# The low half of each weight tile made by an accumulating GpSimd transfer

## The chip, the cores and the metric

The kernel runs on one core of a Trainium2 chip. The metric is device time in microseconds (us). Before the change the median of three runs is 882.69 us (882.68 to 883.96).

## The reference

One decoder layer on x of shape (1, 512, 1024), float32:

```
xn = rmsnorm(h, norm1_gain)
q, k, v, u, gates = split(xn @ w_in)              # 1024+1024+1024+512+2048 columns
o  = diff_attention(rope(rmsnorm(q)), rope(rmsnorm(k)), v)   # 8 heads, causal, softmax - lam*softmax
attn_branch = (rmsnorm(o) * 0.8) @ w_attn_proj
s  = s5_layer(u, ...)                             # 32 groups, state 64, scan over 512 tokens, GLU
ssm_branch = s @ w_ssm_proj
h  = h + (g_attn * attn_branch + g_ssm * ssm_branch) @ w_out     # gates through a sigmoid
hn = rmsnorm(h, norm2_gain)
gate, val = split(causal_dwconv(hn @ w_up))       # 2 x 2816 columns, convolution of width 3
h  = h + (silu(gate) * val) @ w_down
```

## The kernel before

Every large product is done in three passes of TensorE, so that float32 accuracy is kept with the fast `float32r` type. An operand a is split into a high half, a rounded to `float32r`, and a low half, a minus that. The product is then high times high, low times high and high times low (`mm3`, lines 536 to 539). Activations are split by `split` (lines 541 to 543); weights are split by `split_w` (lines 520 to 528), which is what changes here.

A weight comes from HBM in pieces of 512 KB, 128 partitions by 1024 floats (four pieces of `w_down` are 256 KB). `load_raw` (508 to 518) takes a buffer from a ring of three (`wr`) and issues one DMA on SyncE's queue. `split_w` takes a buffer from a ring of four for the high half (`wh`) and one from a ring of four for the low half (`wl`). Then:

```
S.copy(hi, raw)
V.tensor_sub(lo, raw, hi.bitcast(F32))
```

ScalarE (S) writes the high half with a rounding copy. VectorE (V) subtracts it from the raw piece and writes the low half. The raw buffer is free for the next load when the subtraction is done; the buffers of the halves are free when TensorE has used them. There are 134 pieces: 44 of `w_in` (the first two of q and of k, split at lines 658 and 660, come first in the kernel), 2 of the GLU, 4 of `w_ssm_proj`, 8 of `w_attn_proj`, 8 of `w_out`, 44 of `w_up` and 24 of `w_down`.

The layer runs in this order, with much overlap: norm 1 and the first projections (up to about 90 us); the state-space layer, its constants and the first attention heads (about 90 to 230 us), where GpSimd does the products of `s5_const`, `s5_chunk`, the rotary step and the inverse square roots, and VectorE the scans, the softmax steps and many eliminations of PSUM; the other heads and the gates (to about 410 us); the mixing and `w_out` (to about 515 us); the gated feed-forward with its convolution (to about 765 us); and `w_down`.

The order is not written by hand. `Schedule` records every operation with its engine, its price (`price`) and what it depends on; `solve` (320 to 419) is a list scheduler that plays the engines through with these prices, and picks on each engine, among the operations whose inputs and buffers are ready, the one with the longest tail plus a constant for its phase (`boost`, lines 465 to 474). `emit` writes the instructions in that order. On the chip each engine works through its own list in order, so an instruction whose input is late holds up all that stands behind it on its engine. The queue of SyncE carries all loads and stores; GpSimd issues no DMA before the change. `shared_port` tells the planner which GpSimd and VectorE operations exclude each other.

Of the kernel before, what the change touches and what calls it, by code (L numbers as in the profile page):

```python
# [8 lines left out]
F32 = mybir.dt.float32  # L9
F32R = mybir.dt.float32r  # L10
AF = mybir.ActivationFunctionType
ALU = mybir.AluOpType
# [68 lines left out]

class Op:
    __slots__ = ("lock", "eng", "calls", "cost", "preds", "succs", "tiles", "alloc", "prio", "npred", "ready", "idx", "start",
                 "end", "nbytes", "phase", "tail", "left", "sim")


class Schedule:
# [3 lines left out]
           "POOL": {"POOL": 30.0, "DVE": 60.0, "ACT": 75.0, "PE": 150.0}}  # L91
    DMA_BW = 355.0
    COLD = 16500.0

    def __init__(self, nc):
        self.nc = nc
# [59 lines left out]
    def _init(self, o, eng):  # L156
        o.eng, o.calls, o.cost, o.preds, o.succs, o.tiles, o.alloc = eng, [], 0.0, {}, [], set(), []
        o.nbytes = 0
        o.lock = False
        o.phase = self.phase  # L160
        o.idx = len(self.ops)
# [85 lines left out]
    @staticmethod  # L247
    def shared_port(eng, fn, out, ins):

        if eng == "POOL":  # L250
            return fn != "memset"
        if eng != "DVE":
            return False
        sb = sum(1 for x in ins if not str(x.space).endswith("PSUM") and x.free_size() > 1)
        return sb > 1 or (sb == 1 and fn in ("tensor_copy", "tensor_scalar"))
# [8 lines left out]
    def price(self, eng, fn, out, ins, acc, o):  # L264
        n = 1
        for x in out.shape[1:]:
            n *= x
        if eng == "PE":
            if fn == "transpose":
                return 109.0  # L270
            if ins[-1].dtype == F32R:
                c = max(0.4167 * n + 13.5, 98.0 if tuple(ins[0].ap)[-1][0] == 1 else 246.0)

                return c if ins[0].shape[0] > 64 else c / 2
            return 1.667 * n + 11 if out.shape[0] > 32 else 55.0
        ps = any(str(x.space).endswith("PSUM") for x in ins)
        ptr = sum(1 for x in ins[1:] if x.free_size() == 1 and n > 1)
        if eng == "ACT":
            return (50 if ps else 92) + 0.833 * n + 93 * ptr + (93 if acc is not None else 0)
        if eng == "DVE":  # L280
            if fn == "reciprocal":
                return 67 + 8 * n
            if fn == "tensor_tensor_scan":
                return 68 + 2.083 * n
            if fn == "tensor_reduce":
                m = 1
                for x in ins[0].shape[1:]:
                    m *= x
                return 68 + 1.042 * m
            ops = sum(1 for x in ins if x.free_size() > 1 or n == 1)  # L290
            if fn in ("tensor_copy", "tensor_scalar", "memset") and not ps:
                return 68 + 0.521 * n
            ptr = sum(1 for x in ins[1:] if x.free_size() == 1) if fn == "scalar_tensor_tensor" else 0
            return 68 + 1.042 * n + (60 if ptr else 0)
        if eng == "POOL":
            if any(v is ALU.pow for v in [o.calls[-1][2].get("op")]):
                return 300 + 165 * n
            if fn == "memset":
                return 36 + 0.84 * n
            if fn == "tensor_copy":  # L300
                return 120 + 3.35 * n
            return 150 + (1.66 if out.shape[-1] <= 16 else 2.1) * n
        o.nbytes += n * out.shape[0] * 4
        return 460.0


    def rank(self):
        for o in self.ops:
            for p in o.preds:
                p.succs.append(o)  # L310
        for o in reversed(self.ops):
            dur = o.cost + (1900.0 + o.nbytes / self.DMA_BW if o.eng == "SP" else 0.0)
            o.tail = dur + max([s.tail + self.lat(o, s) for s in o.succs], default=0.0)

    def lat(self, a, b):
        if a.eng == "SP":
            return 0.0
        return self.LAT[a.eng].get(b.eng, 130.0)

    def solve(self):  # L320
# [5 lines left out]
        left = {t: t.left for o in ops for t in o.alloc}  # L326
# [29 lines left out]
        now = 0.0  # L356
        while done < len(ops):
            if not events:
                self.stuck(ops, avail, waiting, can, used, tagused)
            now = heapq.heappop(events)  # L360
            while events and events[0] <= now + 1e-6:
                heapq.heappop(events)
            while pend and pend[0][0] <= now + 1e-6:
                _, _, o = heapq.heappop(pend)
# [5 lines left out]
            for e in engs:  # L370
                if free_at[e] > now + 1e-6:
                    continue
                w = waiting[e]
                while w and w[0][0] <= now + 1e-6:
                    _, i = heapq.heappop(w)
                    heapq.heappush(avail[e], (-ops[i].prio, i))
                hold = []
                pick = None
                while avail[e]:
                    pr, i = heapq.heappop(avail[e])  # L380
                    if can(ops[i]):
                        pick = ops[i]
                        break
                    hold.append((pr, i))
                for h in hold:
                    heapq.heappush(avail[e], h)
                if pick is None:
                    if w:
                        heapq.heappush(events, w[0][0])
                    continue  # L390
                o = pick
                for t in o.alloc:
                    used[t.cls] = used.get(t.cls, 0) + 1
                    tagused[t.tag] = tagused.get(t.tag, 0) + 1
                    nxt[t.cls] = max(nxt.get(t.cls, 0), t.seq + 1)
                o.start = now
                cost = o.cost * (2.0 if e == "PE" and now < self.COLD else 1.0)
                if o.lock:
                    cost += max(0.0, port - now)
                    port = now + cost  # L400
                free_at[e] = now + cost
                o.end = now + cost
                if e == "SP":
                    dma_free = max(now + 1100.0, dma_free) + o.nbytes / self.DMA_BW
                    o.end = dma_free + 900.0
                heapq.heappush(events, free_at[e])
                heapq.heappush(events, o.end)
                heapq.heappush(pend, (o.end, o.idx, o))
                for s in o.succs:
                    s.npred -= 1  # L410
                    r = o.end + self.lat(o, s)
                    s.ready = max(s.ready, r)
                    if s.npred == 0:
                        heapq.heappush(waiting[s.eng], (s.ready, s.idx))
                        heapq.heappush(events, s.ready)
                order.append(o)
                done += 1
# [21 lines left out]
def build(tc, A, out, dbg=None):  # L439
# [11 lines left out]
    def bc(ap, shape):  # L451
# [10 lines left out]
    sch.caps = {"X": 10, "N": 19, "C": 29, "T": 8, "Z": 15, "S": 18, "G2": 23, "sT": 25, "g": 10, "R": 26,  # L462
        "rope": 33, "P": 15, "AT": 15, "O": 8, "pmm": 3, "pa": 2, "px": 1, "po": 1, "p5": 4, "pu": 4, "pq": 9, "pb": 7}

    sch.boost = {"": 6384700, "c0": -125100, "c1": -423900, "c2": 861800, "c3": -573000, "down0": 4913100,
# [5 lines left out]
        "s3": 5910300, "ssm": -676100, "swk": 2750200, "swq": -2342100, "tables": 482600, "u": 1182300,  # L471
# [3 lines left out]
    sch.fifo = set(sch.caps) | {"wr", "wh", "wl", "F", "cv", "h", "mS", "hr"}  # L475
    sch.dram = {"hbuf": {}, "sbuf": {}}

# [39 lines left out]
            raws.append(raw)  # L517
        return raws

    def split_w(raws):  # L520
        res = []
        for raw in raws:
            hi = sch.new_tile(wpool.tile(list(raw.shape), F32R, tag="wh", name=nm("wh"), bufs=4), "wh", "wh")
            lo = sch.new_tile(wpool.tile(list(raw.shape), F32R, tag="wl", name=nm("wl"), bufs=4), "wl", "wl")
            S.copy(hi, raw)
            V.tensor_sub(lo, raw, hi.bitcast(F32))
            res.append((hi, lo))
        return res

# [110 lines left out]
    for t in range(NT):  # L640
# [14 lines left out]
            split(xh[c], xl[c], pb.rearrange("p (k n) -> p k n", k=4))  # L655
        if t == 1:
            sch.phase = "swq"
            w_q = split_w(raw_q)
    sch.phase = "swk"
    w_k = split_w(raw_k)  # L660

    sch.phase = "tables"

# [769 lines left out]
```

## Time and profile before

| What | Value |
|---|---|
| median of three runs | 882.69 us |
| the profiled execution's own time | 883.83 us |
| its span, first to last instruction | 882.1 us |
| TensorE matmul (PE) busy | 853.6 us, 97% |
| VectorE (DVE) busy | 585.9 us, 66% |
| ScalarE (ACT) busy | 363.8 us, 41% |
| GpSimd (POOL) busy | 181.9 us, 21% |
| DMA engines, mean busy share | 32% |
| granted TensorE clock, mean | 0.992 |

A busy time is the time in which at least one instruction of that engine ran. The clock is the share of full speed that was granted to TensorE; it is either full or half at any moment. The share of the DMA engines is a mean over the core's 16. Since every operation is emitted at line 436, rows are told apart by their tiles: `wr`, `wh` and `wl` are the raw piece and its halves, `pb` a PSUM bank, `s_S` and `s_T` the work tiles of the state-space layer, `k` its constants, `s_P` the softmax tiles, `s_cv` the convolution tiles of the feed-forward.

### The profile page before, as it was taken

Reading aid. Unit: us, or ns where it says so; the run is one execution under the profiler, and the core shown is the slowest. Engines: PE = TensorE matmul, PEld = TensorE weight load, DVE = VectorE, ACT = ScalarE, POOL = GpSimd, SP = SyncE. Lnnn points to the kernel's source line nnn. Section 1 sums busy time; section 2 is a strip of 40 time slices with the busy share of each in tenths; the row PEclk is TensorE's granted clock in tenths of the full one; section 3 lists DMA queues with packets and bytes.
Section 4 is the critical chain, followed back from the end, with each engine's and each line's share of the span. In section 5 each row is a group of like instructions: output and inputs, shape, how many; then the busy total and the mean of one; then the engine's idle time right before and its main releaser. Section 6 shows DMA issues by size and latency. Waiting matters only on the chain.

```text
span 882.1 us, 12703 instructions
## 1 busy us (share of the span) xinstructions
PE 853.6 (97%) x4922; PEld 738.9 (84%) x4922; DVE 585.9 (66%) x1129; ACT 363.8 (41%) x703; POOL 181.9 (21%) x169
## 2 busy tenths in 40 slices
PE   5999899989899999999999999999999999999998
PEld 3998679979679989888889988888888888888887
DVE  4668999899995788864444532599877777324322
ACT  5325462643552466654132531464444444213210
POOL 2445686226103304200000000012211111000000
PEclk9999999989999999999999999999999999999999
DMA  9131113113142301228332652433333333322321
GB/s 286 31 117 49 49 48 94 51 49 97 50 137 91 115 17 49 72 71 273 100 100 85 207 171 76 118 95 96 96 96 95 96 98 99 103 69 86 119 84 59
DMA packets 113208, 85.95 MB, mean 97 GB/s; under 512 B 9634, under 2 KB 99322, under 8 KB 113148
## 3 DMA queue, kind: packets, MB, share of 16 engines
q1 hardware_dynamic: 113148, 85.14, 31.6%
q8 instruction: 38, 0.62, 0.3%
q14 instruction: 22, 0.18, 0.1%
HBM read 78.84 MB, written 6.29 MB: 97 GB/s over the span
## 4 chain that ended last, share of the span: by engine, by line
PE 83%; DVE 10%; ACT 3%; issue 2%; DMA 1%; SPq 1%; POOL 0%; DVEq 0%; ACTq 0%
PE pb L436 83%; DVE s_S L436 4%; DVE wl L436 1%; DVE k L436 1%; DVE s_P L436 1%; DMA s_X<-in_x 1%; ACT s_P L436 1%; DMA wr<-in_w_in 1%; DVE s_rope L436 1%; SPq L436 1%; DVE ml L436 1%; ACT s_G L436 0%; ACT k L436 0%; DVE s_G L436 0%; ACT s_g L436 0%
## 5 line engine op out<-in xcount | busy, mean ns | idle before, releaser
L436 ACT CAST wh<-wr 128x1024 fp32r<-128x1024 f32 (+1 forms) x134 | 139.2, 1039 | 330.1 <-PE pb L436 290.6
L436 DVE TENSOR_TENSOR wl<-wr,wh 128x1024 fp32r<-128x1024 f32 (+1 forms) x134 | 172.3, 1290 | 153.0 <-ACT wh L436 152.6
L436 PE MATMUL pb<-hh,wh 128*128 128x512 f32 (+1 forms) x368 | 140.4, 382 | 0.9 <-ACT wh L436 0.9
L436 PE MATMUL pb<-hh,wl 128*128 128x512 f32 (+1 forms) x368 | 139.8, 380 | 0.0
L436 PE MATMUL pb<-hl,wh 128*128 128x512 f32 (+1 forms) x368 | 139.8, 380 | 0.0
L436 PE MATMUL pb<-wh,xh 128*128 128x256 f32 (+1 forms) x416 | 125.7, 302 | 0.0
L436 PE MATMUL pb<-wh,xl 128*128 128x256 f32 (+1 forms) x416 | 122.2, 294 | 0.1
L436 PE MATMUL pb<-wl,xh 128*128 128x256 f32 (+1 forms) x416 | 122.0, 293 | 0.0
L436 POOL TENSOR_TENSOR s_cv<-s_cv,s_cv 128x512 f32<-128x512 f32 x22 | 37.6, 1707 | 263.1 <-DVE s_cv L436 235.9
L436 PEld LDWEIGHTS pb<-wh,xh 128*128 128x128 f32 x416 | 84.3, 203 | 2.9 <-issue 1.0
L436 PEld LDWEIGHTS pb<-wh,xl 128*128 128x128 f32 x416 | 84.3, 203 | 0.7 <-DVE xl L436 0.4
L436 PEld LDWEIGHTS pb<-wl,xh 128*128 128x128 f32 x416 | 84.2, 202 | 0.0
L436 PEld LDWEIGHTS pb<-hh,wh 128*128 128x128 f32 x368 | 69.2, 188 | 14.2 <-ACT wh L436 1.0
L436 PEld LDWEIGHTS pb<-hh,wl 128*128 128x128 f32 x368 | 69.2, 188 | 13.4 <-issue 0.2
L436 PEld LDWEIGHTS pb<-hl,wh 128*128 128x128 f32 x368 | 69.2, 188 | 13.2
L436 PE MATMUL pb<-wh,s_F 128*128 128x512 f32 (+1 forms) x252 | 71.5, 370 | 0.0
L436 DVE SCALAR_TENSOR_TENSOR s_cv<-s_cv,cw,s_cv 128x511 f32<-128x511 f32 (+1 forms) x88 | 67.7, 805 | 0.0
L436 POOL TENSOR_TENSOR s_T<-k 128x256 f32<-128x256 f32 (+1 forms) x48 | 48.8, 1049 | 22.9 <-DVE k L436 22.9
L436 PEld LDWEIGHTS pb<-wh,s_F 128*128 128x128 f32 x252 | 45.4, 188 | 8.6
L436 PE MATMUL pb<-xh,wh 128*128 128x512 f32 x128 | 52.6, 411 | 0.0
L436 ACT ACTIVATE s_P<-s_P,mx,rq 128x128 f32<-128x128 f32 (+3 forms) x64 | 41.3, 649 | 24.1 <-DVE mx L436 24.1
L436 PE MATMUL pb<-xl,wh 128*128 128x512 f32 x128 | 50.1, 392 | 0.0
(207 smaller groups left out, 1632.1 us busy)
## 6 DMA issues: line engine op xcount, KB each, us to landing
wr<-in_w_in SPq DMA_DIRECT2D x44, 512.0 KB
wr<-in_w_up SPq DMA_DIRECT2D x44, 512.0 KB
wr<-in_w_down SPq DMA_DIRECT2D x20, 512.0 KB
wr<-in_w_attn_proj SPq DMA_DIRECT2D x8, 512.0 KB
wr<-in_w_out SPq DMA_DIRECT2D x8, 512.0 KB
s_X<-in_x SPq DMA_DIRECT2D x8, 256.0 KB
wr<-in_w_ssm_proj SPq DMA_DIRECT2D x4, 512.0 KB
sbuf<-s_g SPq DMA_DIRECT2D x8, 256.0 KB
```

Of the source, the lines that this page charges most:

```text
L436: getattr(e, fn)(*a, **k)
```

## The change

The low half is made in two steps for 130 of the 134 pieces. ScalarE, right behind the high half, writes the negated high half into the low half's buffer: the raw piece times -1, rounded in the same way. GpSimd then issues a DMA that adds the raw piece, in place, onto that buffer. VectorE's subtraction is gone there. The four first pieces of q and k keep it (`split_w(..., False)`). The planner gets a price for the new operation: 1.1 us of GpSimd to issue it, and 3.5 us more until the data has landed; its loads are planned as if the new transfers took nothing from the DMA engines. All phase constants are different, so the order of the whole kernel is drawn anew. Rings and sizes are the same.

```diff
-    def split_w(raws):
+    def split_w(raws, dma=True):
         ...
             S.copy(hi, raw)
-            V.tensor_sub(lo, raw, hi.bitcast(F32))
+            if dma:
+
+                S.mul(lo, raw, -1.0)
+                G.dma_start(lo, raw, accum_op=ALU.add)
+            else:
+                V.tensor_sub(lo, raw, hi.bitcast(F32))
...
-            w_q = split_w(raw_q)
+            w_q = split_w(raw_q, False)
...
-    w_k = split_w(raw_k)
+    w_k = split_w(raw_k, False)
...
+    ADD_ISSUE = 1100.0
+    ADD = 3500.0
...
-            return fn != "memset"
+            return fn not in ("memset", "dma_start")
...
         if eng == "POOL":
+            if fn == "dma_start":
+                o.post = self.ADD
+                return self.ADD_ISSUE
...
-                o.end = now + cost
+                o.end = now + cost + o.post
...
-    sch.boost = {"": 6384700, "c0": -125100, "c1": -423900, "c2": 861800, "c3": -573000, "down0": 4913100,
...
+    sch.boost = {"": 3729900, "c0": 18900, "c1": -112300, "c2": -298700, "c3": -1460600, "down0": 5137100,
...
```

## Rows read from the trace of the kernel before

**Rows 1.** Page, part 1: busy us of each engine, share of the span, instructions.
```profile
PE 853.6 (97%) x4922; PEld 738.9 (84%) x4922; DVE 585.9 (66%) x1129; ACT 363.8 (41%) x703; POOL 181.9 (21%) x169
```

**Rows 2.** All engines in four stretches of the span.
```profile
core 0: us, PE busy (x) PEld busy (x) DVE busy (x) ACT busy (x) POOL busy (x), PEclk, DMA share, GB/s
...
92.40:228.70 136.30, 123.11 (x883) 110.21 (x881) 129.03 (x224) 60.69 (x137) 73.83 (x72) 0.96 0.22 66
...
564.70:882.10 317.40, 313.17 (x1437) 260.46 (x1435) 196.21 (x239) 116.57 (x144) 37.55 (x22) 1.00 0.30 93
...
0.00:20.00 20.00, 9.74 (x36) 6.44 (x36) 8.53 (x12) 10.58 (x19) 3.92 (x14) 1.00 0.94 304
...
862.00:882.10 20.10, 16.75 (x97) 14.51 (x96) 4.23 (x7) 1.24 (x2) 0.00 (x0) 0.97 0.14 53
```

**Rows 3.** What PE waited for between 92.4 and 228.7 us: total, times, longest.
```profile
PE pb L436 <- DVE s_S L436: 5.8, 5, 1.9
PE pb L436 <- DVE s_P L436: 2.4, 1, 2.4
```

**Rows 4.** PE alone: stretch, its length, busy (count), granted clock, DMA share, GB/s.
```profile
175.00:180.00 5.00, 2.71 (x23) 1.00 0.00 0
180.00:185.00 5.00, 3.19 (x14) 0.62 0.00 0
```

**Rows 5.** Low halves on DVE: stretch, its length, busy (count), clock, DMA share, GB/s.
```profile
92.40:228.70 136.30, 22.25 (x16) 0.96 0.22 66
...
470.20:860.00 389.80, 91.44 (x69) 1.00 0.34 105
```

**Rows 6.** Page, part 5: groups with busy us, mean ns of one, idle before.
```profile
L436 ACT CAST wh<-wr 128x1024 fp32r<-128x1024 f32 (+1 forms) x134 | 139.2, 1039 | 330.1 <-PE pb L436 290.6
L436 DVE TENSOR_TENSOR wl<-wr,wh 128x1024 fp32r<-128x1024 f32 (+1 forms) x134 | 172.3, 1290 | 153.0 <-ACT wh L436 152.6
```

**Rows 7.** Timeline of ACT (start, duration): a high half in the state-space stage.
```profile
175.86 1.05 ACT L436 CAST wh<-wr 128x1024 fp32r<-128x1024 f32 x1 [0.25 <-PE pb L436]
```

**Rows 8.** Timeline of DVE: the low half of that same piece.
```profile
199.42 1.22 DVE L436 TENSOR_TENSOR wl<-wr,wh 128x1024 fp32r<-128x1024 f32 x1
```

**Rows 9.** Timeline of the feed-forward: high halves, a low half, the next load.
```profile
642.39 1.05 ACT L436 CAST wh<-wr 128x1024 fp32r<-128x1024 f32 x1 [1.72 <-PE pb L436]
...
643.48 1.82 DVE L436 TENSOR_TENSOR wl<-wr,wh 128x1024 fp32r<-128x1024 f32 x1 [0.41 <-ACT wh L436]
...
645.33 11.24 SPq L436 DMA_DIRECT2D wr<-in_w_up  x3
...
647.79 1.05 ACT L436 CAST wh<-wr 128x1024 fp32r<-128x1024 f32 x1 [2.92 <-PE pb L436]
...
658.67 1.05 ACT L436 CAST wh<-wr 128x1024 fp32r<-128x1024 f32 x1 [2.92 <-PE pb L436]
```

**Rows 10.** Timeline: a load, and the copy that waited for it.
```profile
114.76 3.14 SPq L436 DMA_DIRECT2D wr<-in_w_in  x2
...
118.27 1.05 ACT L436 CAST wh<-wr 128x1024 fp32r<-128x1024 f32 x1 [2.01 <-DMA wr<-in_w_in]
```

**Rows 11.** DMA queue between 640 and 660 us: packets, MB, share of 16 engines.
```profile
q1 hardware_dynamic: 4160, 2.10, 36.0%
```

**Rows 12.** Chain of waits (start, us, what): an early load.
```profile
3.82 5.29 DMA wr<-in_w_in
```

**Rows 13.** Instructions on `wr` (min/median/max ns): one DMA issue on SyncE's queue.
```profile
L436 SPq DMA_DIRECT2D wr<-in_w_up x44: 367/368/385, 483.1 to 721.5; - x44
```

**Rows 14.** Groups of the whole run: POOL's, and one of ACT.
```profile
L436 POOL TENSOR_TENSOR s_T<-k 128x256 f32<-128x256 f32 (+1 forms) x48 | 48.8, 1049 | 22.9 <-DVE k L436 22.9
...
L436 ACT ACTIVATE s_cv<-s_cv,cw 128x512 f32<-128x512 f32 x44 | 35.8, 814 | 18.7 <-DVE s_cv L436 18.7
...
L436 POOL TENSOR_TENSOR dtxe<-ecol,k 128x16 f32<-128x16 f32 x1 | 3.3, 3345 | 1.8 <-DVE qss L436 1.8
```

**Rows 15.** DVE between 92.4 and 228.7 us: tensor-scalar steps on SBUF tiles.
```profile
L436 DVE TENSOR_SCALAR s_S<-s_S 128x512 f32<-128x512 f32 x8 | 3.4, 419 | 0.3 <-ACT s_S L436 0.3
```

More of the change, by code (lines that the diff above doesn't have):

```diff
@@ L83 @@
     __slots__ = ("lock", "eng", "calls", "cost", "preds", "succs", "tiles", "alloc", "prio", "npred", "ready", "idx", "start",
-                 "end", "nbytes", "phase", "tail", "left", "sim")
+                 "end", "nbytes", "post", "phase", "tail", "left", "sim")
 class Schedule:
@@ L158, in _init @@
         o.nbytes = 0
+        o.post = 0.0
         o.lock = False
@@ L311, in rank @@
         for o in reversed(self.ops):
-            dur = o.cost + (1900.0 + o.nbytes / self.DMA_BW if o.eng == "SP" else 0.0)
+            dur = o.cost + o.post + (1900.0 + o.nbytes / self.DMA_BW if o.eng == "SP" else 0.0)
             o.tail = dur + max([s.tail + self.lat(o, s) for s in o.succs], default=0.0)
     def lat(self, a, b):
-        if a.eng == "SP":
+        if a.eng == "SP" or a.post:
             return 0.0
@@ L463, in build @@
         "rope": 33, "P": 15, "AT": 15, "O": 8, "pmm": 3, "pa": 2, "px": 1, "po": 1, "p5": 4, "pu": 4, "pq": 9, "pb": 7}
-    sch.boost = {"": 6384700, "c0": -125100, "c1": -423900, "c2": 861800, "c3": -573000, "down0": 4913100,
[5 rows of a table removed]
-        "s3": 5910300, "ssm": -676100, "swk": 2750200, "swq": -2342100, "tables": 482600, "u": 1182300,
[3 rows of a table removed]
+    sch.boost = {"": 3729900, "c0": 18900, "c1": -112300, "c2": -298700, "c3": -1460600, "down0": 5137100,
[5 rows of a table added]
+        "s3": 5370100, "ssm": 199700, "swk": 2188400, "swq": -3373700, "tables": 1028600, "u": 2523400,
[3 rows of a table added]
     sch.fifo = set(sch.caps) | {"wr", "wh", "wl", "F", "cv", "h", "mS", "hr"}
```

16 rows, old and new, of the table psum are left out of this document.

## The prediction

> **What bounds the kernel now.** I read the page's first part, then busy times by stretch, then what PE waits for, then the timelines. PE is busy 853.6 us of a span of 882.1 [rows 1], so 28.5 us are all that PE ever idles. The stretches say where: 10.3 us in the first 20, where the first loads come in; 3.4 us in the last 20, after the last matmul; 13.2 us between 92.4 and 228.7 [rows 2]. Everywhere else together there are 1.6. From 564.7 us on, feed-forward and `w_down`, PE idles 4.2 us, nearly all in the tail, and no faster VectorE helps there.
>
> The stretch from 92.4 to 228.7 us is the one that the change can reach. There DVE is busy 129.0 of 136.3 us, POOL 73.8 and ACT 60.7 [rows 2]. PE's waits are for DVE: 5.8 us on state-space tiles, 2.4 on softmax tiles, the rest in smaller ones down to 0.6 [rows 3]. They cost a second time: between 175 and 180 us PE is busy 2.71 us of 5, between 180 and 185 it is granted a mean clock of 0.62, which is half speed (1.2 GHz) for most of those 5 us [rows 4]. Over the stretch the mean is 0.96, so 0.04 x 136.3 = 5.5 us of full-speed work are lost. Waits and clock together are 18.7 us: that is what a free DVE could give back here.
>
> Weights are no bottleneck of PE, only of DVE. The high half copied at 175.86 us [rows 7] gets its low half at 199.42 [rows 8]: the rings keep their order, and each is the 24th of its kind. For 23.6 us the subtraction stood in DVE's queue and the raw buffer was held.
>
> **The change, part by part.** *Removed:* 130 subtractions. All 134 take 172.3 us, 1.29 each [rows 6]. In the stretch there are 16 of them, 22.25 us [rows 5], 1.39 each since POOL gets in their way. DVE falls from 129.0 to 106.8 us, 78% of the stretch, below PE's 123.1. From 470 to 860 us, 69 of them with 91.4 us [rows 5] go as well, worth nothing: PE runs without gaps there.
>
> *What the removal gives:* at most 18.7 us (waits and clock), at least 0 (if DVE's chains are a matter of latency). DVE loses more time than PE waits, 22.25 against 13.2, but spread over the stretch, and a wait shrinks only by what stood ahead of it; scans, eliminations and GpSimd products still come one after the other. I take 10, a little over half. What is late next is then the state-space chain itself, with POOL's products in it.
>
> *Added on ACT:* 130 negations, of the shape of the copy, 1.04 us [rows 6]; from above, a scaled activation on half the columns takes 0.81 [rows 14], so 1.63. I take 1.05, since no scale has to be fetched: 137 us in all, ACT from 364 to 500 of 882. In the stretch 60.7 + 16.8 = 77.5 of 136.3; from 564.7 us on 116.6 + 57 x 1.05 = 176 of 317.4. ACT has waited 290.6 us for PE to free a high-half buffer [rows 6], which covers it: 0. Without this cover a weight is 1.05 us later.
>
> *Added on POOL:* 130 issues. The trace of before has none. From below, SyncE's issue, 0.37 us [rows 13]; from above POOL's longest operation, 3.35 [rows 14]. I take 1.1, near POOL's most frequent product of 1.05 [rows 14] (the planner's price is 1.1 too). In the stretch POOL goes from 73.8 to 73.8 + 17.6 = 91.4 of 136.3. Each issue also waits for ACT's negation, and behind it in POOL's list stand the products and inverse square roots of the state-space layer and the rotary step; after 564.7 us it is the gate products, 37.6 us in all [rows 2]. Where ACT is late, these wait too. I take 0, with both cases in the rivals.
>
> *Added on the DMA engines:* 130 transfers of 512 KB that read raw piece and destination and write the destination. Four loads, 2.10 MB, take 36.0% of 20 us [rows 11]: 1.8 us of all engines each. Data time for the transfer is then 1.8 (write only counts) to 3.6 (twice the reading). Latency T from POOL's end to landing: a quiet load needs 3.5 us from issue to the copy that waited for it [rows 10], the slowest of the early ones 5.3 [rows 12]. So T is between 1.8 (data alone) and 10.6 (5.3 doubled); I take 4.4, midway between the two loads. In the feed-forward a piece is used every (658.67 - 642.39)/3 = 5.43 us [rows 9]. The engines then work 1.8 + 1.8 to 3.6 = 3.6 to 5.4 of every 5.43 us.
>
> The cover there is the ring of three raw buffers. Today the load is issued at 645.33, as the low half ends, and its copy starts at 658.67 [rows 9]: 16.3 us from the copy at 642.39, of which subtraction and its wait take 2.9 and 13.3 are left for a load of 3.5 to 5.3. Afterwards: copy 1.05, negation 1.05, issue 1.1, T, load. 3.2 + 4.4 + 5.3 = 12.9 of 16.3, so it is hidden, with 3.4 us to spare. If POOL is in the middle of a gate product (37.6 us over 22 of them, 1.7 each), 1.7 remain. Cost: 0.
>
> *Moved:* all phase constants, so the order of everything. It can win at most the 1.6 us of idle elsewhere, and lose as much as half of today's waits in the stretch, 7. I take 0.
>
> **The sum.** The profiled execution took 883.83 us, its span and 1.7 around it. 883.8 - 10 = 873.8. The median of the runs, 882.69, lies 1.1 below, so 872.7; I say 873.
>
> **Two rules that bear on it.** DVE's tensor-scalar steps on SBUF tiles are 8 in the stretch, 3.4 us [rows 15], and DVE as a whole is busy 95% of it. The Trainium skill, "SBUF — State Buffer", section "SBUF: two separate sides", warns that a DMA issued from GpSimd has its descriptors written by GpSimd, which is locked out while VectorE runs certain copies and tensor-scalar steps, and advises issuing elsewhere. Taken strictly it delays at most 8 of 16 issues by 0.42 us; taken for every DVE instruction of some 0.7 us it gives 11 us more on POOL, 103 of 136.3: the sum stays, and the second rival gets 0.03 more than it would have. For the transfer, the rows give a load only. The same skill, "DMA: Bandwidth & Descriptors", section "Anatomy of one DMA — SWDGE (gpsimd) path", fits 2.0 us plus bytes over 436 GB/s, and "Collectives: The Full Stack" puts an adding transfer at half the rate of a copy, for its two reads: an estimate of 2.0 + 2.4 = 4.4 us. No run here shows it; by it the first rival loses some chance and the sum is the same.
>
> **The rivals.**
> 1. *The transfer outlasts the ring* (slower). Decides from T = 16.3 - 3.2 - 3.5 = 9.6 us on, or from 5.43 - 1.8 = 3.6 us of engine time per transfer. At T = 10.6 a ring turn takes 17.3 instead of 16.3: 0.34 us for each of 69 pieces, 23 us. 872.7 + 23 = 896. For it: loads and transfers share the engines, and the new plan doesn't count that. Against: the loads come in packets of some 500 bytes (2.10 MB in 4160 [rows 11]), a transfer moves rows of 4 KB.
> 2. *POOL becomes the bound of the stretch* (slower). POOL has 136.3 - 73.8 = 62.5 us to spare for 16 issues, so it decides at 3.9 us for each, its wait for ACT included. At 4.5: 73.8 + 72 = 145.8, 9.5 over the stretch of today, 892. For it: POOL is in the state-space chain, in order. Against: POOL idles nearly half of the stretch.
> 3. *Nothing comes of it* (no change, 882 to 884). The waits are on state-space and softmax tiles, none on `wl`; if the chains bind by latency, they stay.
> 4. *All of it comes* (faster still): 883.8 - 18.7 - 1.1 = 864. For it: DVE drops under PE everywhere, and a clock that never falls.
>
> **How the numbers follow.** Forecast 0.56, its own range 866 to 879; rivals 0.15, 0.11, 0.10, 0.08 in that order. A difference under 0.2%, 1.8 us, can't be told from none. Faster is forecast and rival 4, 0.64; same is rival 3, 0.10; slower rivals 1 and 2, 0.26. The range goes from rival 4 with 3 us for the new order, 861, to rival 1 with 1 more, 897; beyond lie transfers slower still and a plan that misfires.
>
> **What would show it.** In the profile after: DVE near 586 - 130 x 1.29 = 418 us; ACT near 500; POOL with some 130 issues of about 1.1 us and few waits behind them; PE's idle in the state-space stage down from 13 to some 5 us and fewer stretches at half clock; the feed-forward with a piece every 5.4 us and no waits of PE for `wl`. Wrong: PE waiting for DMA or `wl` after 470 us (rival 1), POOL full and PE waiting for tiles that it makes (rival 2), or PE's waits on `s_S` and `s_P` as before (rival 3).

## The result, and the profile after

The changed kernel takes 894.14 us (median of 4 runs, 892.94 to 898.42), the one before 883.33 beside it: a ratio of 1.0126 [1.0086, 1.0167]. It is slower by 10.8 us where 10 us of gain were forecast. The profiled execution took 895.16 us.

First the page of after: part 1, two queues of part 3 (packets, MB, share of 16 engines), two groups of part 5 and a DMA issue of part 6 (count, KB, median us from issue to landing).

```profile
PE 856.2 (96%) x4922; PEld 738.7 (83%) x4922; DVE 452.1 (51%) x999; ACT 476.5 (53%) x833; POOL 286.3 (32%) x299
...
q0 software_dynamic: 18720, 67.12, 42.4%
q1 hardware_dynamic: 113148, 85.14, 31.1%
...
L443 ACT ACTIVATE wl<-wr 128x1024 fp32r<-128x1024 f32 (+1 forms) x130 | 136.1, 1048 | 275.4 <-PE pb L443 251.7
L443 POOL DMA_DIRECT2D wl<-wr x130 | 113.7, 877 | 449.3 <-ACT wl L443 396.2
...
wl<-wr POOLq DMA_DIRECT2D x126, 512.0 KB, 5.7
```

DVE is busy 133.8 us less than in [rows 1]. The subtractions were 167 of that (172.3 of 134 [rows 6], 4.9 of the four that are left), so its other steps are busy 34 us longer. ACT has gained 112.7 (the records of a negation and the copy behind it overlap a little). The span is 893.4, so PE idles 37.2 us in place of 28.5. Its busy time, the same matmuls, is 2.6 longer. Now the stages (columns as in [rows 2]):

```profile
92.40:228.70 136.30, 130.27 (x942) 116.16 (x941) 117.35 (x239) 83.89 (x172) 73.98 (x79) 1.00 0.55 125
228.70:410.00 181.30, 175.35 (x1169) 153.05 (x1168) 100.87 (x338) 109.40 (x252) 49.50 (x47) 0.99 0.61 142
410.00:515.00 105.00, 100.80 (x637) 90.83 (x636) 29.01 (x54) 49.13 (x88) 15.03 (x18) 0.98 0.90 228
515.00:765.00 250.00, 246.96 (x1132) 205.60 (x1132) 128.86 (x183) 146.66 (x186) 76.00 (x68) 0.99 0.91 198
```

The first stretch is the one that the prediction argued about: PE idles 6.0 us there, 13.2 before, and its clock is 1.00 instead of 0.96 [rows 2]. The gain is there (the order is new, so the stretch doesn't hold the same work: 942 of PE's matmuls run in it, 883 before). The next three, in which the kernel before idled 1.2 us in all, now idle 6.0, 4.2 and 3.0 at clocks of 0.98 to 0.99. PE's waits in the whole of after say on what (total, times, longest):

```profile
PE pb L443 <- DMA wl<-wr: 15.1, 12, 3.5
PE pb L443 <- DMA ident<-in_cst: 5.3, 1, 5.3
PE pb L443 <- DVE s_rope L443: 3.6, 2, 2.2
...
PE pb L443 <- DVE s_S L443: 0.7, 1, 0.7
```

The state-space waits are down to 0.7 from 5.8 [rows 3]. 15.1 us of waits for the new transfers have come in. They aren't spread evenly: three of them, up to 259, 425 and 536 us, are 3.5, 2.5 and 2.2 us long, and five between 838 and 865 us are 0.35 to 0.68 each. The chain of waits of after has these transfers in it (start, us, what):

```profile
235.34 7.81 DMA wl<-wr
250.79 8.16 DMA wl<-wr
292.27 8.88 DMA wl<-wr
...
528.31 7.30 DMA wl<-wr
...
858.28 6.62 DMA wl<-wr
```

A transfer with no packet of a load beside it takes 4.5 us from the start of its issue to landing (piece 34, 270.54 to 275.06); the median is 5.7, and the longest 9.9 (piece 53, from 419.24). "Pieces" are counted from 0 in the order of splitting.

In the steady feed-forward nothing is lost. The first row is that of all engines, the others are ACT's timeline (start, duration; in brackets its wait):

```profile
640.00:660.00 20.00, 20.00 (x90) 16.53 (x89) 12.01 (x16) 11.42 (x15) 6.01 (x5) 1.00 0.94 202
...
643.18 1.06 ACT L443 ACTIVATE wl<-wr 128x1024 fp32r<-128x1024 f32 x1 [3.44 <-PE pb L443]
...
648.62 1.06 ACT L443 ACTIVATE wl<-wr 128x1024 fp32r<-128x1024 f32 x1 [1.50 <-PE pb L443]
```

A piece comes every 5.44 us, PE is busy 20.00 of 20, and the DMA engines are at 0.94. The brackets matter, as numbers 12 to 14 show. In the order as planned each negation stands ahead of the copy of its own piece, in all 130, so the transfer doesn't wait for the copy. It starts when PE has freed something, and that is the *low-half* buffer which the negation writes. At the end of the kernel the same chain no longer fits:

```profile
843.86 1.06 ACT L443 ACTIVATE wl<-wr 128x1024 fp32r<-128x1024 f32 x1 [4.19 <-PE pb L443]
...
850.37 1.06 ACT L443 ACTIVATE wl<-wr 128x1024 fp32r<-128x1024 f32 x1 [4.52 <-PE pb L443]
```

The second negation is followed by a transfer from 851.73 to 858.35, and PE waits 0.68 us for it. One piece takes 6.5 us here.

The negations of two of the three longest waits, those up to 259 and 536 us (pieces 33 and 70), waited for something else, their load:

```profile
249.44 1.06 ACT L443 ACTIVATE wl<-wr 128x1024 fp32r<-128x1024 f32 x1 [2.30 <-DMA wr<-in_w_in]
...
526.95 1.06 ACT L443 ACTIVATE wl<-wr 128x1024 fp32r<-128x1024 f32 x1 [6.19 <-DMA wr<-in_w_up]
```

Each of these loads was issued less than 0.1 us after the transfer three pieces before it had landed (243.15 and 518.31 us), that is, when the *raw* buffer came free. Of PE's 15.1 us, 5.8 stand behind a negation whose last wait was for PE (pieces 16, 52 and 125 to 129), 7.0 behind one that waited for its load (17, 33 and 70), and 2.2 behind one that waited for neither (39 and 55). So both rings delay transfers. A wait doesn't explain its case alone: the negation of piece 52 waited only 0.47 us, and its transfer took 7.8.

### The profile page after: what moved, and what is told of

It reads as the page before. It is cut to its first block, busy times and chain, and to the rows that moved or that the text cites. A ratio compares the mean times of both kernels' runs of the same rounds, so it can differ in the third digit from the quotient of the medians.

```text
span 893.4 us, 12963 instructions
## 1 busy us (share of the span) xinstructions
PE 856.2 (96%) x4922; PEld 738.7 (83%) x4922; DVE 452.1 (51%) x999; ACT 476.5 (53%) x833; POOL 286.3 (32%) x299
## 3 DMA queue, kind: packets, MB, share of 16 engines
q1 hardware_dynamic: 113148, 85.14, 31.1%
## 4 chain that ended last, share of the span: by engine, by line
PE 67%; DMA 10%; DVE 8%; issue 7%; ACT 4%; POOL 3%; SPq 0%; POOLq 0%; ACTq 0%; DVEq 0%
PE pb L443 67%; DMA wl<-wr 6%; DMA wr<-in_w_in 3%; DVE k L443 2%; DVE s_S L443 2%; ACT wl L443 2%; ACT wh L443 1%; DMA wr<-in_w_up 1%; POOL wl L443 1%; DVE s_P L443 1%; DVE mx L443 1%; DVE s_rope L443 1%; POOL qrs L443 0%; DVE qss L443 0%; POOL dtxe L443 0%
## 5 line engine op out<-in xcount | busy, mean ns | idle before, releaser
L443 ACT ACTIVATE wl<-wr 128x1024 fp32r<-128x1024 f32 (+1 forms) x130 | 136.1, 1048 | 275.4 <-PE pb L443 251.7
L443 POOL DMA_DIRECT2D wl<-wr x130 | 113.7, 877 | 449.3 <-ACT wl L443 396.2
L443 ACT CAST wh<-wr 128x1024 fp32r<-128x1024 f32 (+1 forms) x134 | 136.9, 1023 | 2.9 <-DMA wr<-in_w_in 2.8
L443 DVE TENSOR_TENSOR s_cv<-pb,s_hj 128x512 f32<-128x512 f32 x44 | 29.4, 684 | 153.8 <-PE pb L443 153.8
L443 DVE SCALAR_TENSOR_TENSOR s_cv<-s_cv,cw,s_cv 128x511 f32<-128x511 f32 (+1 forms) x88 | 76.1, 889 | 17.4 <-ACT s_cv L443 17.0
L443 PEld LDWEIGHTS pb<-hh,wl 128*128 128x128 f32 x368 | 69.6, 189 | 15.9 <-DMA wl<-wr 2.6
```

Source lines behind the costliest of these rows:

```text
L443: getattr(e, fn)(*a, **k)
```

## The experiments

The theory at first was that VectorE's relief is real, and that the transfers cost more than it gives. The rivals were that the new order is the loss, that POOL or ACT is, or that the DMA engines are simply full. Pieces are counted as above.

**1. The new order without the transfers.** In the order as planned, each transfer is written out as a subtraction and its negation is left out:

```diff
-  S.mul(lo, raw, -1.0)
-  G.dma_start(lo, raw, accum_op=ALU.add)
+  V.tensor_sub(lo, raw, hi.bitcast(F32))
```

> The changed kernel's order of instructions, with VectorE's subtraction back at the place of each transfer and the negations left out. Theory A (the transfers share the DMA engines with the loads and land later than planned; PE waits for low halves): the 15.1 us of PE waits on transfers go, VectorE is back near 620 us busy, and some of the state-space waits return; 876 to 888 us, below the changed kernel by at least 5. Theory B (the new order costs the time by itself, whatever makes the low half): 890 us or more.

895.15 us (894.59 to 895.89), ratio 1.0125 [1.0102, 1.0148]. PE's waits:

```profile
PE pb L454 <- DVE s_rope L454: 5.3, 4, 4.0
...
PE pb L454 <- DVE s_AT L454: 3.5, 3, 1.8
PE pb L454 <- DVE mx L454: 3.1, 2, 2.6
```

As slow as the change, but with no wait on a low half: PE's new waits are for VectorE, late in an order drawn for a freer one. By itself the new order is a loss of 11.4 us (883.73 beside it); it needs the relief. My 0 for it was no term of its own.

**2. The old order with the transfers.** At the place of 130 subtractions stands nothing; ACT negates right behind the copy, and POOL issues the transfer some 2 us later in the plan.

```diff
+  if id(o) in self.neg:
+      self.nc.scalar.mul(lo, raw, -1.0)
+      due.append((o.start + 2200.0, lo, raw))
```

> The order of the kernel before, with negation and transfer in place of the subtraction for 130 pieces (the negation right behind the copy, the transfer issued 2.2 us of planned time later, at the latest where the subtraction stood). Theory A: transfers of 5 to 10 us under loads make PE wait for low halves here too, 888 to 900 us, slower than before. Theory B: the transfer is harmless and VectorE is relieved, 870 to 883 us.

1026.96 us (1022.83 to 1033.96), ratio 1.1624 [1.1569, 1.1678]; I had not expected it so far off. PE waits 81.9 us for low halves, 34 times, though a transfer takes only 5.3 us in the median and the queue's share is 36.0%. So how often a transfer is late depends on more than its length. The order is another, and here the negation also stands behind the copy of its piece, in after ahead of it; the two weren't separated.

**3. Half of each transfer.** After, but only half the columns are added.

```diff
+  n, c = (n // 2, c) if n > 1 else (n, c // 2)
+  a = (a[0][:, 0:n, 0:c], a[1][:, 0:n, 0:c])
```

> The changed kernel in its own order, but each transfer adds only one half of its piece (the other half of each low half stays the negated high half, so the result differs); negations, issues and waits are as in the changed kernel. Theory A: a transfer lands in about 3.3 to 4.5 us from its start instead of 5.7, PE waits for low halves fall from 15.1 to under 4 us, DMA share in the feed-forward from 0.93 to about 0.65; 872 to 884 us, which also tells what relief VectorE gives. Theory B: 890 us or more, since the order is the same.

875.16 us (872.52 to 875.96), ratio 0.9891 [0.986, 0.9923]. Transfers take 3.4 us and 22.8% of the engines, PE waits 1.6 us on low halves. So relief and order together are worth at least 8.6 us (883.73 beside it), close to the 10 forecast, and the second half of the transfers costs 19.

**4. The relief in the old order alone.** As 2, for the 22 pieces from 8 to 29, those of the state-space stage.

```diff
-  if n >= 4:
+  if 8 <= n < 30:
```

> As the second kernel, but with transfers only for the 22 pieces of the state-space stage (gates of the state-space branch, the first v, the second heads' q, k and v, the GLU and its projection); all others keep the subtraction. Theory A: few loads run in this stage, transfers land in about 4.5 us, VectorE loses some 25 us of work there; PE's waits for VectorE between 92 and 229 us fall from 13 to about 6 and nothing is lost later: 873 to 880 us. If VectorE's relief is worth nothing (its chains bind by latency): 881 to 885 us.

908.29 us (907.04 to 908.83), ratio 1.0271 [1.0248, 1.0295]: a miss. PE waits on DVE's `s_S`, 16.5 us, the longest 10.1, not on transfers. POOL's list stands at issues whose negation is late (`POOL wl <- ACT wl` 62.4 us in all, the longest 9.9), and runs of POOL's products hold VectorE up, as the last section shows. How much each of the two costs was not separated.

**5. Transfers in the first part only.** After, with the subtraction from piece 50 (`w_attn_proj`) on; 46 transfers are left.

```diff
+  if n >= 50:
+      sch.piece[neg] = ("negsub", high, None)
+      sch.piece[add] = ("sub", high, (lo, raw, hi.bitcast(F32)))
```

> The changed kernel's order; transfers for the 46 pieces up to the gates (w_in, the GLU, w_ssm_proj), and VectorE's subtraction in place of negation and transfer for the 84 pieces from w_attn_proj on. Theory A (transfers that share the engines with loads land late, and the relief of VectorE is worth something only in the first half): the waits after 400 us (about 10 us with the clock that falls behind them) go, the relief stays; 876 to 886 us. Theory B (the relief is needed in the feed-forward too): 890 us or more.

882.24 us (878.35 to 888.01), ratio 0.999 [0.9967, 1.0013]: the late transfers cost some 12 us more than subtractions in their place. PE still waits 6.4 us for early ones.

**6. Half by transfer, half by subtraction, in all pieces.**

```diff
+  elif True:
+      sch.piece[neg] = ("neghalf", high, None)
+      sch.piece[add] = ("half", high, (cut(lo, True), cut(raw, True), cut(hi, True).bitcast(F32)))
```

> The changed kernel's order; each low half made half by negation and transfer (256 KB), half by VectorE's subtraction on the other columns: the result is whole. VectorE gets back some 85 us, to about 535. Theory A: transfers land in about 3.4 us as in the kernel with half transfers, PE waits for them under 4 us; 873 to 882 us, faster than before. If VectorE's relief has to be whole to be worth anything: 884 us or more.

888.3 us (887.17 to 889.03), ratio 1.0054 [1.0041, 1.0066], a miss: waits on low halves are down to 1.7, but `s_rope` 4.7, `mx` 3.7 and `s_AT` 2.2 are back. DVE is busy 528.2 us, and half the relief isn't enough for this order.

**7 and 8. Are the DMA engines the limit?** In 7 the loads read rows of 4 KB (other data); in 8 the planner is told 0.88 us of issue, 3.7 to landing and 2.9 us of the engines for each transfer, with the same constants.

```diff
-            load(raw, src[:, :, h * (nc_ // 2):(h + 1) * (nc_ // 2)] if cols
...
+                load(row, w[(k0 + h) * P:(k0 + h + 1) * P, at:at + m])
```

> The changed kernel, transfers whole and in the same order, but most weight pieces are loaded as contiguous rows of 4 KB from another place of the matrix (so the result differs), not as 512-byte to 2 KB rows: same bytes, fewer packets, so that loads take less of the DMA engines. If sharing with the loads is what makes the transfers late: from start to landing below 5.3 us instead of 5.7, PE waits for low halves below 8 us, 880 to 889 us. If the transfer's own length does it: PE waits as before, 891 to 896 us.

```diff
-    ADD_ISSUE = 1100.0
-    ADD = 3500.0
+    ADD_ISSUE = 880.0
+    ADD = 3700.0
...
+                    dma_free = max(now + cost + 500.0, dma_free) + o.nbytes / 180.0
```

> The changed kernel with a planner that counts what the trace shows: 0.88 us to issue, 3.7 us to land, and 2.9 us of the DMA engines for each transfer, which loads and transfers then wait for. Same phase constants, so the order is drawn anew. If the waits come from a plan that leaves no room: PE waits for low halves under 8 us and 878 to 889 us. If the order as such is not the matter, or the constants fit only the old plan: 890 us or more.

891.52 us (888.44 to 897.16) and 894.94 us (893.1 to 896.21); ratios 1.0099 [1.0065, 1.0132] and 1.0128 [1.0112, 1.0145]. A third of the packets took the loads' share from 31.1 to 29.1% only, so 7 did not free the engines and says little; transfers take 5.6 us and PE's waits for low halves are 15.9. A plan that knows the price waits 11.3 us for low halves, its longest 7.3: with these constants and rings, knowing the price didn't help.

**9. Half the loads.** After, with loads of half a piece; negation and transfer read that half twice, so that a transfer moves as much as before.

```diff
+  if o.eng == "SP":
+      a = (cut(a[0]), cut(a[1]))
+  else:
+      a = (pairs(a[0]), twice(a[1])) + tuple(a[2:])
```

> The changed kernel in its own order with its transfers whole (512 KB), but of 130 weight pieces only half is loaded, and copy, negation and transfer read that half twice (so the result differs). If sharing the DMA engines with the loads makes the transfers late: from start to landing falls from 5.7 toward the 4.5 us that a transfer without a load beside it takes in the changed kernel, PE waits for low halves from 15.1 to under 6 us, 876 to 886 us. If the transfer's own length is all: 4.5 us is not reached, PE waits stay above 10 us, 889 us or more.

891.79 us (888.49 to 892.5), ratio 1.0091 [1.007, 1.0112]. Loads land in 3.1 us and their share falls to 18.8%, but transfers still take 5.6 and PE still waits 12.1. It speaks against "the engines are too full", but not cleanly: the transfers read twice took twice the packets (35360) and POOL 1.22 us to issue.

**10 and 11. Choosing the pieces.** 10 is number 5 with the subtraction from piece 26 on. 11 is number 5 with the subtraction also for the four pieces at which PE waited there (0.2, 1.3, 3.4 and 1.5 us).

```diff
-  if n >= 50:
+  if n >= 26:
```

> As the second kernel, but transfers only for the 22 pieces from number 4 to 25 (up to the GLU), and subtractions for all later ones. If VectorE's relief counts only up to some 230 us: 874 to 881 us. If the attention stage from 230 to 400 us, whose order was drawn for a free VectorE, needs it too: 882 to 890 us.

```diff
-  if n >= 50:
+  if n >= 50 or n in (16, 17, 33, 39):
```

> The changed kernel's order; VectorE's subtraction in place of negation and transfer for the 84 pieces from w_attn_proj on, and for the four earlier ones for which PE waited 1.5 to 3.6 us (numbers 16, 17, 33 and 39); transfers for the other 42. If PE's waits for late transfers are the whole loss: the 6.4 us of waits that stood in the kernel with 46 transfers go, with the clock that falls behind the longest; 873 to 879 us, faster than before. If other pieces then turn late, or four subtractions hold up VectorE: 880 us or more.

885.84 us (884.82 to 886.3) and 879.53 us (878.09 to 880.88); ratios 1.0028 [1.0018, 1.0039] and 0.9952 [0.9937, 0.9967]. The attention heads need the relief too. 11, just above the 879 expected and with one wait of 1.6 us left, is the first version with whole results that is ahead of the kernel before; it takes 3.6 us of the 10.

**12 to 14. The rings.** What made a transfer late was still open: its length, the engines, or the buffers. After in its own order, the planner counting as before, with a fourth raw buffer (12), a fifth low-half buffer (13), or both (14, where two steps of the convolution on VectorE change places; else the instructions of all three come in the order of after). The room comes from the 2 KB work slots.

```diff
-NSLOT = 43
+NSLOT = 41
...
-            raw = sch.new_tile(wpool.tile(shape, F32, tag="wr", name=nm("wr"), bufs=3), "wr", "wr")
+            raw = sch.new_tile(wpool.tile(shape, F32, tag="wr", name=nm("wr"), bufs=4), "wr", "wr")
```

> The changed kernel in its own order, with a fourth raw buffer (41 in place of 43 of the 2 KB work slots make room; the planner goes on counting three). Theory A (what starts a transfer too late is the ring of four low-half buffers: the negation waits until TensorE has freed one, and only then can the transfer go; raw pieces are there in time): loads start a piece earlier, TensorE's waits for the low halves stay at 10 us or more, 890 to 896. Rival B (the raw buffer, held until the transfer has landed, makes the loads late): waits under 6 us, 881 to 887. Rival C (the DMA engines have no time left for loads and transfers in the tight places): waits and time as after the change, 890 to 898, here and with the larger low-half ring.

```diff
-            lo = sch.new_tile(wpool.tile(list(raw.shape), F32R, tag="wl", name=nm("wl"), bufs=4), "wl", "wl")
+            lo = sch.new_tile(wpool.tile(list(raw.shape), F32R, tag="wl", name=nm("wl"), bufs=5), "wl", "wl")
```

> The changed kernel in its own order, with a fifth low-half buffer in place of the fourth raw one (41 work slots; the planner goes on counting four). Theory A (the low-half ring starts the transfers too late): a negation can go one piece earlier, 5 to 6 us, as much as a whole transfer takes; TensorE's waits for low halves fall from 15.1 to under 5 us, 880 to 886. Rival B (raw ring): waits stay, 890 to 896. Rival C (engines too busy): waits stay, 890 to 898.

> The changed kernel with the fourth raw buffer and the fifth low-half buffer (39 work slots; the order of some convolution steps on VectorE in the feed-forward is another). Theory A: as with the low-half buffer alone, 879 to 886. Rival B: as with the raw buffer alone, 881 to 887. If each ring hides a part: below both, 874 to 880. Rival C: 890 to 898.

| | us | ratio | PE waits for low halves |
|---|---|---|---|
| 12, raw ring 4 | 887.93 (884.32 to 889.41) | 1.0037 [1.0013, 1.0061] | 10.4 |
| 13, low ring 5 | 889.0 (878.46 to 891.8) | 1.0034 [1.0, 1.0068] | 7.7 |
| 14, both | 872.61 (871.45 to 875.1) | 0.9874 [0.9852, 0.9895] | 3.9 |

The profiled execution of 13 took 884.03 us, less than its median, so its waits may be a little low. Neither ring alone is what its theory asked for; both together give more than the 874 that I had put as the best case. The negations' groups show why. First 12, then 13, then 14, with the copies of 14 (mean ns; then the idle time of ACT ahead of them, and what ended most of it):

```profile
L443 ACT ACTIVATE wl<-wr 128x1024 fp32r<-128x1024 f32 (+1 forms) x130 | 136.0, 1047 | 272.9 <-PE pb L443 260.3
```

```profile
L443 ACT ACTIVATE wl<-wr 128x1024 fp32r<-128x1024 f32 (+1 forms) x130 | 135.5, 1043 | 40.3 <-DMA wr<-in_w_up 17.3
```

```profile
L443 ACT ACTIVATE wl<-wr 128x1024 fp32r<-128x1024 f32 (+1 forms) x130 | 135.5, 1043 | 16.9 <-DMA wr<-in_w_in 8.9
...
L443 ACT CAST wh<-wr 128x1024 fp32r<-128x1024 f32 (+1 forms) x134 | 138.7, 1037 | 221.2 <-PE pb L443 217.9
```

With four low-half buffers the negations wait for PE to free one, 251.7 us in all in after and 260.3 in 12. With five, 3.7 us of that are left, and they wait for loads, which can't start until a raw buffer is free, and that is held until the transfer has landed. With four raw buffers as well, little of either is left. ACT still waits for PE, 217.9 us, but ahead of the copies, and a negation no longer stands behind that wait. PE's single waits agree: of the seven of 12, five stand behind a negation that waited for PE and none behind one that waited for its load; of the three of 13, the one of piece 70 stands behind a load and none behind PE. The transfers of 14 are no shorter. Its page and its stages:

```profile
PE 848.6 (97%) x4922; PEld 735.3 (84%) x4922; DVE 445.1 (51%) x999; ACT 479.4 (55%) x833; POOL 282.1 (32%) x299
...
q0 software_dynamic: 18720, 67.12, 42.7%
...
wl<-wr POOLq DMA_DIRECT2D x126, 512.0 KB, 5.8
```

```profile
92.40:228.70 136.30, 132.59 (x954) 117.83 (x953) 115.77 (x244) 86.37 (x178) 71.83 (x78) 1.00 0.56 130
228.70:410.00 181.30, 178.45 (x1194) 155.67 (x1192) 97.43 (x329) 113.68 (x261) 51.12 (x50) 1.00 0.66 159
410.00:515.00 105.00, 103.13 (x666) 94.03 (x667) 31.30 (x61) 51.83 (x87) 16.14 (x19) 0.98 0.89 218
515.00:765.00 250.00, 249.12 (x1124) 207.00 (x1123) 122.79 (x171) 145.70 (x177) 74.06 (x67) 1.00 0.89 202
```

5.8 us to landing, 42.7% of the engines, shares of 0.89 in the same stages: the transfers cost as much and are as long as in after, and PE idles 22.0 us in place of 37.2. So the same length and the same load on the engines cost little once there is room to issue the transfers ahead, as half the length cost little with the old rings (number 3): what cost time was the length against that room. In the last product ACT shows it at once:

```profile
836.91 1.06 ACT L443 ACTIVATE wl<-wr 128x1024 fp32r<-128x1024 f32 x1
841.58 1.05 ACT L443 CAST wh<-wr 128x1024 fp32r<-128x1024 f32 x1 [3.61 <-PE pb L443]
842.53 1.06 ACT L443 ACTIVATE wl<-wr 128x1024 fp32r<-128x1024 f32 x1
847.20 1.05 ACT L443 CAST wh<-wr 128x1024 fp32r<-128x1024 f32 x1 [3.61 <-PE pb L443]
```

Negations no longer wait, the copy does; a piece takes 5.62 us, not 6.5.

**15 and 16. Are larger rings a gain by themselves?** The same two rings in the kernel before (two swaps in its order at the start of the last product), and in number 1, the new order with subtractions.

```diff
-NSLOT = 43
+NSLOT = 39
...
-            raw = sch.new_tile(wpool.tile(shape, F32, tag="wr", name=nm("wr"), bufs=3), "wr", "wr")
+            raw = sch.new_tile(wpool.tile(shape, F32, tag="wr", name=nm("wr"), bufs=4), "wr", "wr")
...
-            lo = sch.new_tile(wpool.tile(list(raw.shape), F32R, tag="wl", name=nm("wl"), bufs=4), "wl", "wl")
+            lo = sch.new_tile(wpool.tile(list(raw.shape), F32R, tag="wl", name=nm("wl"), bufs=5), "wl", "wl")
```

> The kernel before with four raw and five low-half buffers (39 work slots; its order is the same but for two swaps among the steps at the start of the last product). Theory A (the larger rings cover the transfers, and with subtractions there is nothing to cover, since TensorE never waited for a low half): 880 to 885, within 0.3% of before. Rival D (larger rings are worth as much without the transfers, because a raw piece may then wait longer for VectorE): 870 to 878.

> The changed kernel's order with the subtraction on VectorE in place of negation and transfer, and with four raw and five low-half buffers: all of the version that measured 872.6, but the transfers. Theory A (transfers give relief, rings cover them, both are needed): VectorE is as late as with the small rings; TensorE waits for its tiles; 888 to 896. Rival D (the rings alone): 870 to 878. In between, each has its part: 879 to 887.

884.22 us (881.87 to 887.52), ratio 1.0013 [0.9995, 1.0031], and 892.04 us (891.84 to 892.35), ratio 1.0103 [1.008, 1.0125]. PE's waits of 16:

```profile
PE pb L454 <- DVE s_rope L454: 5.5, 4, 4.1
...
PE pb L454 <- DVE s_AT L454: 3.2, 3, 1.7
...
PE pb L454 <- DVE mx L454: 2.2, 2, 1.8
```

Without the transfers the rings give nothing in the old order, and 3.1 us in the new one (895.15 to 892.04, intervals that overlap), which stays behind the kernel before. In the new order relief and rings are needed together: 872.61 us, 11.3 under the kernel before beside it (883.92). The old order with the transfers and both larger rings was not run, so that the new order is needed once the rings are larger isn't shown.

## Why the prediction was wrong

- **The relief of VectorE (10 of at most 18.7): right, a little small.** In the stretch of [rows 2] PE's idle time fell by 7.2 us and its clock rose from 0.96 to 1.00, worth the 5.5 us of the working: 12.6. Between 175 and 185 us, half idle and at half clock before [rows 4], PE is now busy throughout. With rings that cover the transfers the whole kernel gained 11.3, and 872.61 stands beside the 873 forecast. That it fits so closely is luck in part: it is another kernel than the one forecast, PE idles 9.5 us less in the stretch, and 4.4 more between 228.7 and 515 us, a loss that the sum didn't have.
- **DVE near 418: wrong, 452.** The subtractions went as forecast, but the other steps are busy 447.2 us in place of 413.6. Number 1, the same order without the transfers, has 433.3, so some 20 us came with the order and some 14 with the transfers. In the stretch DVE stays at 117.4 us, not 106.8.
- **ACT (364 to 500; mean 1.05): right,** 476.5 and 1.048. **POOL's issue (1.1): right, a little large,** 0.877, and 1.18 at most. Its waits for ACT, taken at 0, cost nothing visible in after; in the old order they are 62.4 us and may be a part of the loss (number 4).
- **The transfer's size: right.** From POOL's end to landing 5.7 - 0.88 = 4.8 us in the median, taken as 4.4, up to 9.1. Data time is 0.424 x 893.4 / 130 = 2.9 us of all engines, in the range of 1.8 to 3.6. The Trainium skill's fit ("DMA: Bandwidth & Descriptors", section "Anatomy of one DMA — SWDGE (gpsimd) path", with the half rate of "Collectives: The Full Stack", section "The bandwidth ceiling: the fold count and why AG ≠ RS ≠ AR") gave an estimate of 4.4 us; a transfer without a load beside it landed 3.6 us after POOL's end (271.39 us) and 4.5 after its start, so the trace agrees to within what that start leaves open.
- **"The cover there is the ring of three raw buffers ... Cost: 0": this step failed.** It looked at the steady feed-forward only, and there it was right: PE 20.00 of 20. Elsewhere the load was late after all: that of piece 70 took 8.6 us from its issue (518.38) to its negation, where the sum had 5.3. And it asked only whether the *load* would be late. Before, a low half was ready some 3 us after its copy began (copy, then a subtraction of 1.2 to 1.8 [rows 6, 9]); now negation, issue and transfer take some 7 (1.05 + 0.3 + 5.7), 11.3 for piece 53 (from 417.89 to 429.18), and they begin only when PE has freed a low-half buffer. That ring of four stands in the section on the kernel before, and in none of my sums. Worse, I took ACT's 290.6 us of waiting for PE [rows 6] as cover for the negation. It was the opposite: a wait of the same kind now stands ahead of the transfer, 251.7 us of it, and delays it. The price is 894.14 - 872.61 = 21.5 us. By the two profiled spans (22.8) it is 15.2 us more idle time of PE, 11.2 of them in waits for low halves (15.1 against 3.9), and 7.6 us more busy time for the same matmuls, at a mean clock of 0.992 against 0.998.
- **"Moved: 0": wrong as a term of its own.** The new order alone costs 11.4 us (number 1), and with the relief it belongs to the gain (numbers 3 and 14). Relief in the old order, with the small rings, lost time (numbers 2 and 4).
- **Rival 1** came near in time (896) and in kind, with a chance of 0.15, and for a wrong reason. It was to decide from 9.6 us to landing or 3.6 us of engine time, in the feed-forward, on the raw ring. Neither was reached in the median, and the steady feed-forward held. Its sign, PE waiting for `wl` after 470 us, did come: six of the twelve waits, 5.2 us. **Rival 2** (POOL full) and **rival 3** (waits on `s_S` as before) did not happen.

What stays open: why some transfers take 8 to 10 us. Those of 512 KB that have packets of the loads' queue and another transfer beside them take 5.9 us in the median (93 of 126), those with neither 4.6 (only 5), but number 9, with half the loads, left the median at 5.6.

## What to carry to other kernels

When a short step on an engine is replaced by a longer one with the same buffers, write down for each ring the time from "buffer free" to "needed again" and put the whole new chain into it, at the stage changes and in the tail as well as in the steady loop; the ring of the *destination* counts as much as that of the source. A wait that already stands ahead of the step is no cover for it: the step starts when that wait ends. If one more buffer helps little, look at which ring the step waits for next before giving the theory up: two rings in series show their worth only together (here 6.2 and 5.1 us alone, 21.5 together).

## What the runs showed of the hardware

A VectorE operation on two SBUF tiles was held up for far longer than its work while POOL ran products back to back. In after, 16 such products of `s_T` tiles on VectorE take 684 ns in the median (min/median/max):

```profile
L443 DVE TENSOR_TENSOR k<-s_T,s_T x16: 674/684/5209, 71.9 to 180.3; 64x512 f32<-64x512 f32 x8, 128x512 f32<-128x512 f32 x8
```

One took 5.21 us, from 72.92 on, and POOL's timeline has, at that time:

```profile
72.57 0.88 POOL L443 DMA_DIRECT2D wl<-wr  x1 [4.27 <-PE pb L443]
73.18 4.39 POOL L443 TENSOR_TENSOR s_T<-k 128x512 f32<-128x512 f32 x4
```

It ended at 78.13, and POOL's four products at 77.57. In number 4 it was two additions of VectorE and six products of POOL (VectorE's timeline, then POOL's):

```profile
112.13 7.95 DVE L449 TENSOR_TENSOR s_S<-s_S,s_S 128x508 f32<-128x508 f32 x2
...
113.44 5.49 POOL L449 TENSOR_TENSOR s_T<-k 128x256 f32<-128x256 f32 x6
```

In the kernel before, the same two additions took 2.77 us. Being held up like this came with the transfers: in the four kernels without them (before, and numbers 1, 15 and 16) no VectorE instruction on the tiles takes more than 2.3 us, and in each of the others two to seven take 2.5 to 8.1. A run of products alone doesn't do it. In number 1, the order of after without the issues, POOL has this:

```profile
108.70 12.28 POOL L454 TENSOR_TENSOR s_T<-k 128x256 f32<-128x256 f32 x12
```

VectorE gets its turn in between: none of its instructions of that time takes more than 1.6 us. The two runs shown here stand right behind an issue on POOL, but not all do, and why VectorE isn't let in is open. That the products are what held it is read from the coincidence of the two timelines.
